# Output projection of a hybrid attention block: the second half of a row block's work comes one row block later, and the late rows' steps sit at earlier positions

## The chip, the cores and the metric

The kernel runs on one core of one Trainium2 chip, in one launch. A core has a matrix engine (TensorE, PE in the profile), three elementwise engines (VectorE is DVE, ScalarE is ACT, GpSimd is POOL) and a queue engine, SyncE (SP), which issues nearly all DMAs of this kernel. Each engine works through its own instruction list in order; semaphores tie the lists together. The metric is the device time of the whole launch in microseconds, lower is better.

## The reference

One layer of a pre-norm residual trunk over 2048 tokens of width 1024: an input projection, two groups of attention heads (four differential heads, eight stick-breaking heads), an output projection with a residual, and a SwiGLU feed-forward of width 2816 with a residual.

```python
u = rms_norm(h, norm1_w[l])
proj = jnp.einsum('bsd,de->bse', u, w_in[l])
dq, dk, dv, sq, sk, sv = jnp.split(proj, SPLIT_POINTS, axis=-1)
...
y_diff = rms_norm(y_diff, diff_out_norm_w[l]) * (1.0 - lambda_init)
...
y_sb = rms_norm(stick_breaking_attention(sq, sk, sv), sb_out_norm_w[l])
...
h = h + jnp.einsum('bse,ed->bsd', mix, w_out[l])
u2 = rms_norm(h, norm2_w[l])
gate = jnp.einsum('bsd,df->bsf', u2, w_gate[l])
up = jnp.einsum('bsd,df->bsf', u2, w_up[l])
h = h + jnp.einsum('bsf,fd->bsd', jax.nn.silu(gate) * up, w_down[l])
```

The change touches the two lines in the middle: the output projection, and the preparation of `u2` for the feed-forward.

## The kernel before

**Number form.** A float32 matrix product is computed as three float16 products: each operand is split into a high half (the rounded value) and a low half (the rest), and high·high, high·low and low·high are added up in PSUM. In the feed-forward each product of 2×2 blocks is done with seven instead of eight block products. For that the activations need seven combinations of their blocks, each one split in two halves. They are kept in DRAM (`xcd`) and loaded as seven tiles `X`, once for each half of the 2048 rows.

**Order of work.** Tokens are handled in 16 row blocks of 128. The attention is run in eight groups of heads; while the last group's attention runs, the output projection's row blocks are dealt in between (`next(op)`), each as soon as the attention of its rows is finished. After the attention come the row blocks that are left; row blocks 12 to 15 are dealt among the loads of the first feed-forward weights. Then the feed-forward runs in 22 steps, 11 groups of 256 columns (`fg`) for each half of the rows: a gate product, an up product (each a `quad` of seven block products of 12 matmuls), and after every few steps a `down` product.

The order in each engine's list is not the program's order. A scheduler simulates the engines and gives each engine, among the instructions whose inputs are ready in its simulation, the one with the highest priority; priority is the place in the program, with offsets (`PRI`; the attention's stages are moved 200 places forward, `ox` and `po` not at all). `tc.issue_after(ins)` adds an edge of order alone: the instructions made inside the block that run on the same engine as `ins` come behind it in that engine's list. Other engines are not bound by it. `note` and `pick` keep a running account of load and choose the engine of a cast or a subtraction.

**A row block of the output projection** (`out_proj`, from L816). The 2·8 halves of the mix rows are loaded (`mt`, L819) and the residual row too (`xf`, L824). Two PSUM banks `po` (a pool of two) take 48 matmuls each, in two parts of 24 (L832). After each 24, VectorE reads the part and adds it to `xf` (L835): these four instructions are the "bank reads". The row goes to DRAM (`hd`, L837).

**`post(t, xf)`** (L848), for row blocks 0 to 11. It takes two tiles of `z4` for each pair of row blocks (a ring of ZB = 9 tiles of 4 KB a partition, which the attention's stages use too, two tiles a stage). Then: norm of the row (ScalarE squares with a running sum L226, a mean L155 on VectorE, a power on POOL L156, a product on VectorE L229); eight PE transposes into two PSUM banks of the attention's tag `sc` (L665) and two ScalarE copies back (L853); and, on odd row blocks, `x_ops` for the pair: the block combinations and splits (casts L89 or L93, subtractions L98), put in `s16` tiles (a ring of three, shared with the attention's splits) and stored to `xcd` (L238), four stores a pair.

**The late rows.** Row blocks 12 to 15 do not pass through `post`. Their norm, transposes and combinations are done during the first two feed-forward steps by a generator, `build_x` (L1189), which works in 15 segments. One call of `tick` runs one segment. The first, called ahead of the steps, reads row blocks 12 and 13 back from `hd` (L1203). Then come, for the pair (12, 13): the norm, the transposes (L1213, L1214), the first put, the combinations, the second put, the third put, and the fourth put together with the read of row blocks 14 and 15; and then the same seven for the pair (14, 15). The split halves stand in a tile `b16` that belongs to the tag `act` (two tiles). The other `act` tile takes the first step's activations, and the second step's activations need the one that `b16` gives back.

`late_at` (L1256) says at which positions of the steps 0 and 1 a segment is run. Position s = 1 to 7 is behind the s-th block product of the gate, 8 to 14 behind the products of up:

```python
def row(s):
    if i < 2 and s in late_at[i]:
        tick(1)
```

In a `quad`, the read of the fourth block product (L1057, tile `c22`) must be done before the seventh, which adds to the same PSUM bank `pd`. Weights of the next step are loaded and split meanwhile (L89 to L221, L954 to L964, tiles `wg`, `wu`, `wd`, staging tile `stages`).

Of the kernel before, what the change touches and what calls it, by code (L numbers as in the profile page):

```python
# [16 lines left out]
ALU = mybir.AluOpType  # L17
# [4 lines left out]
S, D, P = 2048, 1024, 128  # L22
# [37 lines left out]
def block(tc, a, out):  # L60
    nc = tc.nc
    PE, ACT, DVE, POOL, SP = nc.tensor, nc.scalar, nc.vector, nc.gpsimd, nc.sync
    top = ExitStack()
    with top:
# [8 lines left out]
        def note(e, ns):  # L73
            load[e] += ns * KW[e]
# [25 lines left out]
        def pri(k):  # L100
            def deco(f):
                @functools.wraps(f)
                def g(*args):
                    with tc.high_priority(PRI[k]) if PRI[k] else nullcontext():
                        return f(*args)
                return g
            return deco

        def nm(s):
            uid[0] += 1  # L110
            return f"{s}{uid[0]}"
# [38 lines left out]
        def rstd(dst, ss, mul, eps):  # L150
            n = dst.shape[-1]
            if n > 1:
                ACT.activation(dst, ss, AF.Identity, bias=eps, scale=mul)
            else:
                DVE.tensor_scalar(dst, ss, mul, eps, op0=ALU.mult, op1=ALU.add)  # L155
            POOL.tensor_tensor(dst, dst, mhalf[:, :n], ALU.pow)  # L156
# [67 lines left out]
        def norm_tile(xf, xn, wgt, junk=None):  # L224
            ss = sm.tile([P, 1], F32, tag="xss", name=nm("xss"))
            ACT.activation(xn if junk is None else junk, xf, AF.Square, accum_out=ss[:])  # L226
            rs = sm.tile([P, 1], F32, tag="xrs", name=nm("xrs"))
            rstd(rs[:], ss[:], 1.0 / D, EPS)
            DVE.scalar_tensor_tensor(xn, xf, rs[:], wgt, op0=ALU.mult, op1=ALU.mult)  # L229

        def x_ops(xn, xt, half, j, bufs, engines="ADP", tte="DP"):
            def put(o, src):
                k = src.shape[1]
                x16 = bufs()
                xv = x16[:, : 1024 * k].rearrange("p (o s n) -> p o s n", o=k, s=2)
                to16(xv[:, :, 0, :], src, 512 * k, engines)
                tt(xv[:, :, 1, :], src, xv[:, :, 0, :], ALU.subtract, 512 * k, tte)
                SP.dma_start(xcd[half][o : o + k, :, j, :].rearrange("o p n -> p o n"), x16[:, : 1024 * k].rearrange("p (o n) -> p o n", o=k))  # L238

            put(0, xn[0])  # L240
            yield
            tt(xt[:, 1], xn[1][:, 1], xn[1][:, 0], ALU.subtract, 512, tte)
            tt(xn[1][:, 0], xn[1][:, 0], xn[0][:, 0], ALU.subtract, 512, tte)
            tt(xt[:, 0], xn[1][:, 1], xn[1][:, 0], ALU.subtract, 512, tte)
            tt(xn[0][:, 0], xt[:, 0], xn[0][:, 1], ALU.subtract, 512, tte)
            yield
            put(2, xn[1])
            yield
            put(4, xt)
            yield  # L250
            put(6, xn[0][:, 0:1])
# [5 lines left out]
        with ExitStack() as ph1:  # L257
# [6 lines left out]
            def z4():  # L264
                return zp.tile([P, 1028], F32, tag="z4", bufs=ZB, name=nm("z4"))
# [396 lines left out]
            def transposed(xn, o):  # L662
                tr = ps.tile([P, 512], F32, tag="sc", bufs=4, name=nm("xtr"))
                for j in range(4):
                    PE.transpose(tr[:, P * j : P * j + P], xn[:, o + P * j : o + P * j + P], id32[:])  # L665
                return tr
# [121 lines left out]
            wos, kos, mts, rp2, spare = [], [], [], [], {}  # L788
# [24 lines left out]
            w2 = bias[:].rearrange("p h n -> p (h n)")  # L813

            def out_proj():
                for t in range(NT):  # L816
                    mt = pp.tile([P, 2 * D], F16, tag="xt", bufs=3, name=nm("mt"))[:].rearrange("p (k n) -> p k n", k=KT)
                    with tc.high_priority(PRI["wm"]) if PRI["wm"] else nullcontext():
                        mts.append(SP.dma_start(mt, ms[t]))  # L819
                    if t in spare:  # L820
                        xf = spare[t].bitcast(F32)
                    else:
                        xf = pp.tile([P, 4, 4, 2, 64], F16, tag="st", name=nm("xf"))[:].rearrange("p c t s e -> p (c t s e)").bitcast(F32)
                    SP.dma_start(xf, x[t * P : (t + 1) * P, :])  # L824
                    for h in range(2):
                        po = psj.tile([P, 512], F32, tag="pj", name=nm("po"))
                        for n in range(2):
                            q = 0
                            sl = slice(256 * n, 256 * n + 256)
                            for kt in range(KT):  # L830
                                for xi, wi in ((0, 0), (0, 1), (1, 0)):
                                    PE.matmul(po[:, sl], lhsT=mt[:, kt, P * xi : P * xi + P], rhs=wos[2 * h + n][wi][:, kt, :], start=q == 0, stop=q == 23)  # L832
                                    q += 1
                            xl = xf[:, 512 * h + 256 * n : 512 * h + 256 * n + 256]
                            DVE.scalar_tensor_tensor(xl, po[:, sl], kos[2 * h + n][:], xl, op0=ALU.mult, op1=ALU.add)  # L835
                    note("D", 1400)
                    SP.dma_start(hd[t], xf)  # L837
                    if t >= 12:
                        yield
                        continue  # L840
                    post(t, xf)
                    yield

            held = []

            @pri("ox")
            def post(t, xf):
                if t % 2 == 0:  # L848
                    held[:] = [z4(), z4()]
                xn = held[t % 2]  # L850
                norm_tile(xf, xn[:, :D], w2)
                for h in range(2):
                    ACT.copy(xn[:, 512 * h : 512 * h + 512], transposed(xn, 512 * h)[:])  # L853
                note("D", 1150)
                note("A", 1000)
                if t % 2 == 1:
                    for _ in x_ops([z[:, :D].rearrange("p (d n) -> p d n", d=2) for z in held], z4()[:, :D].rearrange("p (d n) -> p d n", d=2), t // 8, t % 8 // 2, lambda: s16p.tile([P, 2048], F16, tag="s16", bufs=SB, name=nm("x16"))[:]):
                        pass

            op = out_proj()  # L860
            outs = 0
            advance(NT - LAG0)
# [11 lines left out]
        with ExitStack() as ph2:  # L874
# [378 lines left out]
            units = []  # L1253
            hs = None
            chains = {}
            late_at = ((5, 9, 10, 11, 12, 13), (1, 6, 9, 10, 11, 12, 13, 14))  # L1256
            for i, (half, fg) in enumerate(steps):
                if i == NFG:
                    load_x(1, XL)
# [83 lines left out]
```

## Time and profile before

| | us |
|---|---|
| median of 3 runs | 2685.7 (2677.81 to 2689.95) |
| the profiled execution | 2685.45 |
| its span, from the first instruction to the last | 2683.6 |
| PE busy in the span | 2498.7 (93%) |
| DVE busy | 1937.3 (72%) |
| POOL busy | 1477.3 (55%) |
| ACT busy | 1346.4 (50%) |

All times in the views are microseconds from the start of the span, single instructions' means in ns where said. A row of the timeline gives start, duration, engine, line, operation and tiles, with the idle time before it in brackets and what ended it. A row of the waits gives the engine and line that waited, what released it, the total, how often, and the longest. A row of the windows gives length, then busy time (and count) of PE, PEld, DVE, ACT and POOL, the granted PE clock, the DMA share and GB/s. Row blocks 0 to 11 lie between 1181 and 1386 us, row blocks 12 to 15 between 1386 and 1428, the first feed-forward step from 1428.4 to 1470.2, the second from there to 1518.6.

### The profile page before, as it was taken

The numbers are of one execution on the slowest core, as the hardware profiler recorded it, in microseconds if no ns is written. First come the engines' busy times: TensorE is split into PE (matmuls) and PEld (weight loads), VectorE is DVE, ScalarE is ACT, GpSimd is POOL, SyncE is SP. The second block draws the span as 40 slices with busy tenths as digits, with TensorE's granted clock in tenths as the row PEclk, the third lists the DMA queues.
The fourth block names the chain that finished last, engine by engine and source line by source line (L and its number), as shares of the span: only waits on it lengthen the run. The fifth ranks groups of instructions, "written<-read, shape, count | busy, mean of one in ns | idle before, by whom it ended". The sixth has DMA issues, their size and how long they took to land. (4 is left out here: it accounts for less than half of the span.)

```text
span 2683.6 us, 50578 instructions
## 1 busy us (share of the span) xinstructions
PE 2498.7 (93%) x19628; PEld 1503.2 (56%) x19628; DVE 1937.3 (72%) x3714; ACT 1346.4 (50%) x2487; POOL 1477.3 (55%) x1095
## 2 busy tenths in 40 slices
PE   7998989898988989889989799999999999999999
PEld 4655656577776776557775344444444444444444
DVE  6898879898989889877766968677785544444434
ACT  4665556567978878665644535344362112111121
POOL 2578667767767766546664546565654232322323
PEclk9999999999999999999999999999999999999999
DMA  7778697768999979987897565655648743635532
GB/s 230 204 163 185 140 206 169 179 147 175 198 178 179 180 158 206 212 191 216 216 280 292 205 231 197 255 222 206 243 184 337 301 174 144 235 140 185 196 111 95
DMA packets 619585, 534.41 MB, mean 199 GB/s; under 512 B 480640, under 2 KB 548224, under 8 KB 609104
## 3 DMA queue, kind: packets, MB, share of 16 engines
q1 hardware_dynamic: 617520, 529.09, 69.8%
q8 instruction: 154, 2.52, 0.4%
q0 software_dynamic: 512, 1.36, 0.2%
q14 instruction: 87, 0.71, 0.1%
q10 hardware_dynamic: 1312, 0.72, 0.1%
HBM read 261.08 MB, written 147.32 MB: 152 GB/s over the span
## 5 line engine op out<-in xcount | busy, mean ns | idle before, releaser
L98 POOL TENSOR_TENSOR s<-z,s 128x1024 f16<-128x1024 f32 (+7 forms) x288 | 471.8, 1647 | 145.0 <-ACT s L89 119.5
L507 PE MATMUL sc<-kT,qT 128*128 128x512 f16 (+3 forms) x1520 | 383.9, 355 | 53.8 <-DVE z L623 19.3
L622 DVE TENSOR_TENSOR_SCAN z<-z,sc 128x512 f32<-128x512 f32 (+3 forms) x320 | 352.9, 1112 | 61.7 <-ACT sc L620 37.3
L1138 PE MATMUL pd<-wd,act 128*128 128x512 f16 x1764 | 390.2, 379 | 0.3 <-DVE cg L1071 0.3
L326 PE MATMUL pj<-w,xt 128*128 128x384 f16 x1920 | 354.4, 333 | 14.3 <-ACT raw L375 5.8
L1030 PEld LDWEIGHTS <-wg 128*128 128x128 f16 x1848 | 182.2, 99 | 236.1 <-issue 22.9
L98 POOL TENSOR_TENSOR act<-cg,act 128x512 f16<-128x512 f32 x110 | 145.8, 1333 | 291.9 <-ACT act L1097 179.5
L518 PE MATMUL yp<-v,aT 128*128 128x64 f16 (+1 forms) x4896 | 269.7, 204 | 39.4 <-DMA aT<-s 38.4
L518 PEld LDWEIGHTS <-aT 128*128 128x128 f16 x4896 | 238.2, 99 | 117.6 <-DMA aT<-s 48.5
L1030 PEld LDWEIGHTS <-wu 128*128 128x128 f16 x1848 | 180.6, 98 | 218.4 <-DVE wu L221 3.2
L1138 PEld LDWEIGHTS <-act 128*128 128x128 f16 x1764 | 172.5, 98 | 207.9 <-issue 0.6
L326 PEld LDWEIGHTS <-xt 128*128 128x128 f16 x1920 | 188.2, 100 | 144.5 <-issue 23.4
L89 ACT CAST s<-z 128x128 f16<-128x128 f32 (+7 forms) x215 | 173.1, 809 | 137.5 <-DMA aT<-s 43.3
L98 POOL TENSOR_TENSOR hs<-hs,cu 128x512 f32<-128x512 f32 x99 | 132.0, 1340 | 171.4 <-DVE hs L1144 70.3
L619 ACT ACTIVATE z<-sc,c 128x512 f32<-128x512 f32 (+3 forms) x320 | 210.7, 663 | 28.7 <-PE sc L507 14.4
L1097 ACT CAST act<-cg 128x512 f16<-128x512 f32 x126 | 77.1, 617 | 242.0 <-DVE cg L1103 193.5
L507 PEld LDWEIGHTS <-qT 128*128 128x128 f16 x1520 | 128.7, 99 | 122.5 <-DVE z L623 22.8
L832 PE MATMUL po<-wo,mt 128*128 128x256 f16 x1536 | 181.0, 277 | 14.1 <-DVE xf L835 8.4
L342 PE MATMUL pj<-xt,w 128*128 128x128 f16 x2304 | 177.5, 222 | 6.7 <-DVE v L364 5.7
L1030 PE MATMUL pm<-X,wu 128*128 128x512 f16 x792 | 180.1, 379 | 2.2 <-DVE wu L221 2.2
L1030 PE MATMUL pm<-X,wg 128*128 128x512 f16 x792 | 178.9, 379 | 0.0
L1144 DVE SCALAR_TENSOR_TENSOR hs<-pd,c,hs 128x512 f32<-128x512 f32 x136 | 98.8, 747 | 110.1 <-PE pd L1138 81.8
(267 smaller groups left out, 4739.5 us busy)
## 6 DMA issues: line engine op xcount, KB each, us to landing
xt<-xs SPq DMA_DIRECT2D x112, 512.0 KB, 4.4
hs<-hd SPq DMA_DIRECT2D x68, 512.0 KB, 4.5
hd<-hs SPq DMA_DIRECT2D x56, 512.0 KB, 4.8
split<-wg SPq DMA_DIRECT2D x11, 1792.0 KB, 7.1
split<-wu SPq DMA_DIRECT2D x11, 1792.0 KB, 7.4
split<-wd SPq DMA_DIRECT2D x11, 1792.0 KB, 6.9
wg<-split SPq DMA_DIRECT2D x11, 1792.0 KB, 7.6
wd<-split SPq DMA_DIRECT2D x11, 1792.0 KB, 10.3
```

The source lines that it names most:

```text
L89: ACT.copy(dst, src)
L98: (DVE if e == "D" else POOL).tensor_tensor(dst, a_, b_, op)
L326: PE.matmul(pj[:, :384], lhsT=xv[:, xi, kt, :], rhs=G["w"][:, wi, kt, :], start=n == 0, stop=n == 23)
L342: PE.matmul(o, lhsT=x_ if c == 2 else w_, rhs=w_ if c == 2 else x_, start=n == 0, stop=n == 23)
L507: last = PE.matmul(sc[:, : 128 * w].rearrange("p (t n) -> p t n", n=P), lhsT=G["q"][i // 4][:, a_, i % 4, :], rhs=G["k"][q][:, b_, 0:w, :] ...
L518: PE.matmul(yp[:, y0 : y0 + wd], lhsT=aT[:, a_, :], rhs=v[:, v_ : v_ + wd], start=start and j == 0 and q == 0, stop=stop and j == nb - 1 a ...
L619: ACT.activation(om[:, lo:hi], sc[:, :w], AF.Sigmoid, scale=G["nkz"][:])
L622: DVE.tensor_tensor_scan(ov, ov, sc[:, :w], om[:, hi : hi + 1], op0=ALU.mult, op1=ALU.bypass)
L832: PE.matmul(po[:, sl], lhsT=mt[:, kt, P * xi : P * xi + P], rhs=wos[2 * h + n][wi][:, kt, :], start=q == 0, stop=q == 23)
L1030: front[0] = PE.matmul(ps_[:].rearrange("p (t n) -> p t n", n=P), lhsT=wv[:, wo, wi, 128 * kt : 128 * kt + 128], rhs=X[xo][:, :, xi, kt, : ...
L1138: front[0] = PE.matmul(po[:], lhsT=act[:, ao, xi, 128 * j : 128 * j + 128], rhs=W["d"][:, wo, wi, :], start=start and u == 0 and q == 0, s ...
L1144: DVE.scalar_tensor_tensor(dst, po[:], kd[:], src, op0=ALU.mult, op1=ALU.add)
```

## The change

`post` keeps the norm. The transposes, the copies back and, on odd row blocks, the combinations and splits move into a new function, `post_late`. Row block t, once its own bank reads are traced, runs `post_late(t - 1)` and then `post(t)`; the VectorE instructions of `post_late` are tied behind row block t's last bank read (`seen`). Row block 11 runs its own `post_late` at once behind its `post`. Row blocks 12 to 15 still have neither.

`late_at` puts eleven of the fourteen segments into step 0 (six before) and three into step 1 (eight before), the last at position 4 of step 1 (14 before).

```diff
-                            DVE.scalar_tensor_tensor(xl, po[:, sl], kos[2 * h + n][:], xl, op0=ALU.mult, op1=ALU.add)
+                            seen = DVE.scalar_tensor_tensor(xl, po[:, sl], kos[2 * h + n][:], xl, op0=ALU.mult, op1=ALU.add)
                     note("D", 1400)
                     SP.dma_start(hd[t], xf)
-                    if t >= 12:
-                        yield
-                        continue
-                    post(t, xf)
+                    if 0 < t < 12:
+                        with tc.issue_after(seen.ins):
+                            post_late(t - 1)
+                    if t < 12:
+                        post(t, xf)
+                    if t == 11:
+                        post_late(t)
                     yield
...
             def post(t, xf):
                 if t % 2 == 0:
                     held[:] = [z4(), z4()]
+                norm_tile(xf, held[t % 2][:, :D], w2)
+
+            @pri("ox")
+            def post_late(t):
                 xn = held[t % 2]
-                norm_tile(xf, xn[:, :D], w2)
                 for h in range(2):
                     ACT.copy(xn[:, 512 * h : 512 * h + 512], transposed(xn, 512 * h)[:])
...
-            late_at = ((5, 9, 10, 11, 12, 13), (1, 6, 9, 10, 11, 12, 13, 14))
+            late_at = ((1, 3, 4, 5, 6, 7, 8, 10, 12, 13, 14), (1, 2, 4))
```

## The prediction, on record before the changed kernel was run

> **What bounds the kernel now.** I read the page first, then the busy time by stage, then PE's waits in the stages that the change touches, then the timeline around the longest of them.
>
> ```profile
> span 2683.6 us, 50578 instructions
> PE 2498.7 (93%) x19628; PEld 1503.2 (56%) x19628; DVE 1937.3 (72%) x3714; ACT 1346.4 (50%) x2487; POOL 1477.3 (55%) x1095
> ```
>
> ```profile
> 1181.00:1386.00 205.00, 190.66 (x2031) 160.83 (x2030) 151.07 (x235) 120.50 (x204) 129.63 (x86) 0.97 0.81 211
> 1386.00:1428.20 42.20, 36.73 (x332) 32.16 (x330) 24.71 (x42) 13.28 (x13) 22.97 (x16) 1.00 1.03 400
> 1428.20:1548.50 120.30, 103.20 (x490) 49.09 (x489) 98.61 (x134) 65.87 (x84) 63.72 (x43) 0.94 0.60 216
> ```
>
> PE bounds the kernel, so the change can win only what PE idles, and what it runs slowed, where the change acts. The three stages are row blocks 0 to 11, row blocks 12 to 15, and the feed-forward from its first gate to the end of its third. PE idles 205 − 190.7 = 14.3 us in the first and 17.1 us in the third, where its clock is also lowest (0.94). Its waits there:
>
> ```profile
> PE po L832 <- DVE xf L835: 8.4, 6, 3.7
> PE sc L507 <- ACT z L853: 1.0, 3, 0.5
> ```
>
> ```profile
> PE pd L1030 <- DVE cg L1057: 12.0, 2, 6.2
> PE fsc L963 <- ACT sq L954: 2.7, 1, 2.7
> PE pd L1030 <- DVE cu L1057: 1.4, 1, 1.4
> ```
>
> The first fence is row blocks 0 to 11, the second the feed-forward's start. In both, VectorE is late in freeing a PSUM bank. It is busy 151.1 of 205 us and 98.6 of 120.3 us, so the question is mostly what stands ahead of a bank read in its list.
>
> **The row blocks: what is moved.** These instructions come one row block later:
>
> ```profile
> L665 PE MATMUL xtr<-id,z 128*128 128x128 f32 x96 | 14.2, 274 | 1.4 <-DVE z L229 1.4
> ```
>
> ```profile
> L853 ACT COPY z<-xtr x24: 578/586/626, 1220.6 to 1385.6; 128x512 f32<-128x512 f32 x24
> L238 SPq DMA_DIRECT2D xcd<-x x24: 319/371/1507, 1234.6 to 1399.5; - x24
> L1225 SPq DMA_DIRECT2D X<-xcd x14: 319/382/963, 1382.9 to 2064.1; - x14
> ```
>
> 96 transposes (14.2 us of PE), 24 copies, the casts and subtractions of six pairs, and 24 stores in SP's list. Nothing is removed: all of it stays work and counts as nothing in the sum. What can change is what waits. `issue_after` adds no instruction.
>
> ```profile
> 1266.12 2.29 DVE L98 TENSOR_TENSOR z<-z,z 128x512 f32<-128x512 f32 x1
> 1331.10 1.20 DVE L98 TENSOR_TENSOR x<-z,x 128x1024 f16<-128x1024 f32 x1
> ```
>
> ```profile
> 1234.75 9.12 PE L832 MATMUL po<-wo,mt 128*128 128x256 f16 x82
> 1268.86 10.25 PE L832 MATMUL po<-wo,mt 128*128 128x256 f16 x66 [3.73 <-DVE xf L835]
> 1334.51 2.78 PE L832 MATMUL po<-wo,mt 128*128 128x256 f16 x24 [1.21 <-DVE xf L835]
> ```
>
> A combination of the pair before (2.29 us) ran straight ahead of the bank read for which PE waited 3.73 us. After that wait 66 matmuls took 10.25 us; at 9.12/82 = 0.111 us each they take 7.3, so the slowed clock cost another 2.9. A split (1.20 us) runs ahead of the wait of 1.21. Behind the last bank read such work does no harm: both banks are then just freed, and PE has up to 48 matmuls for one bank, 48 × 0.111 = 5.3 us, before it misses the next. The transposes' wait for the norm (1.4) goes, since the norm is then a row block old. The score matmuls' wait for the copies (1.0) should go too, since the copies need not wait for a norm either. That is at most 3.73 + 2.9 + 1.2 + 1.4 + 1.0 = 10.2 us. The other bank-read waits (8.4 − 4.9 = 3.5 us) have attention's instructions, a norm, or a late load ahead of them, and the norm stays where it was. I take three quarters of 10.2, **7.5 us**, because a list made anew will have new collisions; bounds 13.7 (10.2 and the 3.5) and a loss, priced as the slow rival below.
>
> The Trainium skill (TensorE: Matmul & The Clock Gate, Part 1) says that an idle window of about 3.4 us halves PE's clock until a busy window of that length has passed. By it a long stall costs an estimated 1.7 us on top of itself, where the row gives 2.9; with 1.7 the row blocks' maximum would be 9.0.
>
> Row block 11's two halves now stand close to row block 10's: two more copies (0.59 us each) come ahead of the last pair's work. They lie beside the matmuls of row blocks 12 to 15 (36.7 of 42.2 us PE). I count nothing; without that cover it is 1.2 us. A cast for which `pick` now takes another engine is also off PE's path; the rows above bound the difference by about one subtraction, 1.2 us either way. The stores pass row loads in SP's list, 0.37 us each; a load held up behind one costs that much, and the `X` tiles that need them are first loaded at 1382.9.
>
> **The late rows: what goes.** The last store out of `b16` gives back the tile that step 1's activations need.
>
> ```profile
> 1521.03 0.43 SPq L238 DMA_DIRECT2D xcd<-b  x1
> 1528.07 1.66 ACT L1097 CAST act<-cg 128x512 f16<-128x512 f32 x3 [4.06 <-DMA xcd<-b]
> 1536.18 3.42 DVE L98 TENSOR_TENSOR act<-cg,act 128x512 f16<-128x512 f32 x2
> ```
>
> ```profile
> 1526.15 2.75 PE L1030 MATMUL pa<-X,wg 128*128 128x512 f16 x12
> 1531.59 1.03 PE L963 MATMUL fsc<-sq,ones 128*128 128x256 bf16 x8 [2.68 <-ACT sq L954]
> 1544.04 4.63 PE L1030 MATMUL pd<-X,wg 128*128 128x512 f16 x12 [6.24 <-DVE cg L1057]
> ```
>
> ScalarE stands 4.06 us for that store. Behind it in its list stand the squares of the next weight, for which PE waits 2.68 us; behind the casts stand VectorE's subtractions, and these come ahead of the bank read for which PE waits 6.24 us. After that the matmuls are slowed, 4.63 − 2.75 = 1.9 us. Together 10.8 us. With the last segment at position 4 of step 1 instead of 14, some ten products of 2.6 us earlier, the tile is back before the activations ask for it. I take all **10.8**; the lower bound is nothing, if VectorE's queue and not the tile sets that stall.
>
> **What the late rows cost.** They come into a stretch in which VectorE is already late.
>
> ```profile
> 1485.69 2.04 DVE L229 SCALAR_TENSOR_TENSOR bx<-bx,xrs,bx 128x1024 f32<-128x1024 f32 x1
> 1487.66 3.48 DVE L221 SCALAR_TENSOR_TENSOR wu<-stages,c,wu 128x1024 f16<-128x1024 f32 x2
> 1491.72 0.68 DVE L1057 TENSOR_TENSOR cg<-pd,cg 128x512 f32<-128x512 f32 x1
> ...
> 1506.77 0.68 DVE L98 TENSOR_TENSOR bx<-bx 128x512 f32<-128x512 f32 x1
> 1507.55 2.43 DVE L98 TENSOR_TENSOR bx<-bx,bx 128x512 f32<-128x512 f32 x1
> 1511.38 1.74 DVE L98 TENSOR_TENSOR bx<-bx,bx 128x512 f32<-128x512 f32 x1
> 1515.57 2.29 DVE L98 TENSOR_TENSOR b<-bx,b 128x1024 f16<-128x1024 f32 x1
> ```
>
> ```profile
> 1492.45 4.82 PE L1030 MATMUL pd<-X,wg 128*128 128x512 f16 x12 [5.73 <-DVE cg L1057]
> ```
>
> In step 1's gate PE waits 5.73 us for a read that stands behind a norm and a weight split. The norm leaves that place, but the second pair's combinations, 0.68 + 2.43 + 1.74 + 2.29 = 7.1 us, move from behind this wait to before it. Bounds: +7.1, if all of it lands ahead of the read; −2.0, if only the norm's going is felt. I take half of 7.1, **3.6 us of loss**, because part of it fills gaps that VectorE has in step 0.
>
> How early can they start?
>
> ```profile
> 1437.41 2.58 SPq L1203 DMA_DIRECT2D bx<-hd  x2
> 1471.25 0.41 SPq L1203 DMA_DIRECT2D bx<-hd  x1
> ```
>
> ```profile
> 1447.89 1.06 ACT L226 ACTIVATE bx<-bx 128x1024 f32<-128x1024 f32 x1 [3.05 <-DMA bx<-hd]
> ```
>
> The first pair's rows land at 1447.9, when gate 0 (seven products of some 2.6 us from 1428.4) is over, so positions 1, 3 and 4 of step 0 can bring nothing forward before that; ScalarE already stands 3.05 us for them. Gain and loss begin with the pair's combinations and with the second read (1471.25), which I expect some 5 us earlier. Should the scheduler put the squares further ahead, the gate's ScalarE work stands behind the same landing; PE's next bank is freed by VectorE, so I count nothing, and 3.05 more if that cover is gone. The four stores and two reads of the second pair pass weight loads in SP's list at about 0.4 us each, with the DMA share at 0.60: nothing.
>
> The Trainium skill (SBUF — State Buffer, "SBUF: two separate sides") says that VectorE with two SBUF inputs and GpSimd lock each other out of a shared port for a whole instruction. The same 128x512 subtraction takes 0.68 and 2.43 us in the rows above. By that rule it matters what POOL runs beside the moved work: if all four ran at 0.68 to 1.2 the loss above would be an estimated 2 us less, if each met a POOL instruction it would be as counted.
>
> **The sum.** 7.5 + 10.8 − 3.6 = 14.7 us. The profiled execution took 2685.45, almost the runs' median of 2685.7, so the forecast is 2685.45 − 14.7 = **2671 us**. Its own range, with the row blocks at 4 to 10.2 and the late rows at 3.7 to 10.8, is 2664.5 to 2677.8.
>
> **The rivals.**
> *All of it* (chance 0.16): both stretches lose nearly all idle time: 13.7 from the row blocks, 10.8 from the later stall, and 5.73 + 2.1 (4.82 − 2.75) from the earlier one: 32.3 us, 2653; about 2660 when a quarter stays. For it: VectorE is not full in either stretch (74% and 82%). Against: at 82% it has little room for order to help.
>
> *It does not do what it says* (0.20): the scheduler places by readiness, the transposes were already behind the norm, and the tile is given back early but VectorE's backlog only changes its place. Then the row blocks give half (4), the late rows 4.06 − 7.1 = −3: 2684.
>
> *Slower, by tiles* (0.25): a pair now keeps its two `z4` tiles until a row block later, so that while a pair is combined five of nine are held (two old, one scratch, two new) instead of three, and attention has four, two stages, instead of six, three stages.
>
> ```profile
> L610 DVE COPY z<-z x14: 136/144/146, 1187.9 to 1352.2; 128x1 f32<-128x1 f32 x14
> L608 DVE MEMSET z<- x13: 59/59/59, 1182.8 to 1335.0; 128x1 f32 x13
> ```
>
> 27 stages start between 1182.8 and 1352.2, one per 6.5 us. If each of the four pairs combined in that time costs attention one stage, that is 26 us; half covered by PE's row matmuls, 13. The row blocks then gain nothing, the late rows keep 7.2: 2691 to 2704, likeliest 2700 since the row blocks still to come need the attention's rows. It decides once score matmuls wait longer for PE than the 5.3 us that a bank covers. For it: the ring is shared. Against: no row of before shows a wait for a `z4` tile, and the new pair's norm can wait a row block.
>
> **How the numbers follow.** Forecast 0.39, all 0.16, nothing 0.20, slower 0.25. A measurement of this kernel tells 0.5% from no change: 2672.3 and 2699.1. Faster: 0.16 + 0.25 of the forecast's 0.39 = 0.41. Slower: 0.21 of the 0.25. Same: 0.38. The range, 2653 to 2702, reaches from the full gain to the middle of the slow rival and leaves out some 0.15.
>
> **What would show it.** In the changed profile: PE's wait for L835 in the row blocks at 5 us or less, with no L98 straight ahead of a bank read; transposes with no wait for L229; the last `xcd<-b` issued before 1510, no wait of ScalarE for it, and the wait of 6.24 gone; the wait of step 1's gate up by about 3.6. Wrong would be: PE waiting for scores or for `aT` by 10 us or more in the row blocks (the tiles), or a wait at L1057 that grows by over 7.

## The result, and the profile after

| | median (us) | range of the runs | runs |
|---|---|---|---|
| before | 2682.27 | 2677.81 to 2689.95 | 5 |
| changed | 2697.81 | 2691.70 to 2700.85 | 5 |

The ratio, taken over the single runs and not from the two medians, is 1.0048, with a 95% interval of 1.0032 to 1.0063: slower by 12.9 us (8.6 to 16.9). The medians lie 15.5 us apart. The forecast was 2671, so the sign is wrong. The time stands inside the range, near its slow end.

The profiled execution of the changed kernel took 2691.70 us, the lowest of its five; that of before took 2685.45, above its median. The two traces therefore show 6.3 us of the difference. Most of what is missing lies ahead of the change: the first matmul of row block 0 (L832) starts at 1176.7 us in the changed kernel's trace and at 1181.3 in before's, though nothing ahead of it was changed. Over the fourteen traces of this document it starts between 1174.0 and 1185.5. Counted from that matmul to the end, the pair shows 10.9 us. From L853 on the changed kernel's lines are 6 higher: L1057 is now L1063, L1213 is L1219, L954 is L960.

The page of the changed kernel first, then its busy time by stage (row blocks 0 to 11; the feed-forward's start), then before's row for the same stretch of the feed-forward:

```profile
span 2689.9 us, 50570 instructions
PE 2492.7 (93%) x19628; PEld 1498.9 (56%) x19628; DVE 1927.6 (72%) x3709; ACT 1348.9 (50%) x2489; POOL 1479.3 (55%) x1098
```

```profile
1181.00:1386.00 205.00, 187.07 (x2010) 157.77 (x2009) 142.22 (x221) 116.11 (x195) 129.32 (x87) 0.98 0.77 208
1430.00:1550.00 120.00, 99.94 (x486) 49.77 (x485) 81.41 (x118) 59.83 (x77) 59.32 (x40) 0.93 0.58 212
```

```profile
1430.00:1550.00 120.00, 102.90 (x487) 48.81 (x486) 97.84 (x128) 67.37 (x84) 63.72 (x43) 0.94 0.60 216
```

In the feed-forward's start VectorE has become much less busy (81.4 of 120 us against 97.8), and still PE idles 20.1 us there, where it idled 17.1. That points away from a VectorE that has too much to do. PE's waits from 1432 to 1560 say what the new idle time is:

```profile
PE xtr L1219 <- DVE bx L229: 11.4, 1, 11.4
PE pd L1036 <- DVE cg L1063: 7.9, 2, 4.1
...
```

One wait of 11.4 us is new: the transposes of row blocks 12 and 13 wait for the norm. PE's timeline around it, and the other engines' at the same time:

```profile
1437.06 2.75 PE L1036 MATMUL pa<-X,wg 128*128 128x512 f16 x12 [0.67 <-ACT cg L1049]
1451.22 3.74 PE L1219 MATMUL xtr<-id,bx 128*128 128x128 f32 x16 [11.41 <-DVE bx L229]
1454.80 2.75 PE L1036 MATMUL pd<-X,wg 128*128 128x512 f16 x12
...
1476.39 1.91 PE L1219 MATMUL xtr<-id,bx 128*128 128x128 f32 x16
...
1504.02 5.28 PE L1036 MATMUL pd<-X,wg 128*128 128x512 f16 x12 [4.12 <-DVE cg L1063]
...
1548.75 2.75 PE L1036 MATMUL pd<-X,wg 128*128 128x512 f16 x12 [3.81 <-DVE cg L1063]
1551.92 1.46 PE L1144 MATMUL pd<-wd,act 128*128 128x512 f16 x6 [0.42 <-ACT cg L1089]
```

```profile
1440.43 0.86 SPq L1209 DMA_DIRECT2D bx<-hd  x2
1447.88 1.06 ACT L226 ACTIVATE bx<-bx 128x1024 f32<-128x1024 f32 x1 [10.87 <-DMA bx<-hd]
1449.88 1.28 DVE L229 SCALAR_TENSOR_TENSOR bx<-bx,xrs,bx 128x1024 f32<-128x1024 f32 x1 [0.66 <-POOL xrs L156]
```

An engine's timeline is its list, since it issues in that order. PE finishes a product at 1437.06 + 2.75 = 1439.81 and has the sixteen transposes next. The rows are asked for at 1440.43 and have landed by 1447.88, as in before's trace; ScalarE's squares and VectorE's product follow, and PE goes on at 1451.22. The fourth product of the gate (`pd` at 1454.80) stands behind the transposes. It needs neither the rows nor the norm: right behind the transposes it runs with no wait. The stall costs another 3.74 − 1.91 = 1.8 us by the slowed clock, against the second pair's same sixteen. Together 13.2 us.

What the positions give back is in the same rows: the two waits for the fourth product's read are 7.9 us instead of 12.0, the wait of 2.68 for the squares is gone, and the 4.63 us product is back at 2.75. So the first `down` product, at 1548.50 before, begins 3.4 us later and not 13. (The 4.6 us by which this trace's row blocks began earlier had been used up by their end.) The other 2.9 of the traces' 6.3 us come behind it, mostly in one more wait for a fourth product's read after 1560, first the changed kernel, then before:

```profile
PE pd L1036 <- DVE cg L1063: 4.9, 1, 4.9
```

```profile
PE pd L1030 <- DVE cg L1057: 2.7, 1, 2.7
```

PE's waits in the row blocks, 1180 to 1390, of the changed kernel; behind it two rows of the same view of before, that the prediction did not show:

```profile
PE po L832 <- DVE xf L835: 5.3, 6, 1.2
PE sc L507 <- DVE z L623: 4.0, 5, 1.5
PE xtr L665 <- DVE z L608: 2.4, 1, 2.4
PE yp L518 <- DMA aT<-s: 2.3, 2, 1.3
PE xtr L665 <- DVE z L229: 1.9, 2, 1.2
```

```profile
PE sc L507 <- DVE z L623: 1.7, 2, 1.5
...
PE yp L518 <- DMA aT<-s: 0.9, 1, 0.9
```

The bank reads' wait went from 8.4 to 5.3 and the longest from 3.7 to 1.2, as the change is built to do. But the score matmuls now wait 4.0 us for the attention's VectorE work (1.7 before), the transposes 2.4 for an attention instruction (none before), `aT` comes 2.3 us late (0.9). The 3.1 us that the output projection won stand against 2.3 + 2.4 + 1.4 = 6.1 us that the work beside it lost.

### The profile page after: what moved, and what is told of

The parts are those of the page before. It is cut to its first block, busy times and chain, and to the rows that moved or that the text cites. A ratio compares the mean times of both kernels' runs of the same rounds, so it can differ in the third digit from the quotient of the medians.

```text
span 2689.9 us, 50570 instructions
## 1 busy us (share of the span) xinstructions
PE 2492.7 (93%) x19628; PEld 1498.9 (56%) x19628; DVE 1927.6 (72%) x3709; ACT 1348.9 (50%) x2489; POOL 1479.3 (55%) x1098
## 5 line engine op out<-in xcount | busy, mean ns | idle before, releaser
L98 POOL TENSOR_TENSOR s<-z,s 128x1024 f16<-128x1024 f32 (+7 forms) x288 | 469.7, 1640 | 153.5 <-ACT s L89 121.6
L98 POOL TENSOR_TENSOR act<-cg,act 128x512 f16<-128x512 f32 x112 | 147.4, 1325 | 293.9 <-ACT act L1103 181.7
L98 POOL TENSOR_TENSOR hs<-hs,cu 128x512 f32<-128x512 f32 x99 | 132.0, 1340 | 171.4 <-DVE hs L1150 69.7
L832 PE MATMUL po<-wo,mt 128*128 128x256 f16 x1536 | 184.4, 279 | 8.8 <-DVE xf L835 5.3
## 6 DMA issues: line engine op xcount, KB each, us to landing
wd<-split SPq DMA_DIRECT2D x11, 1792.0 KB, 10.8
```

Of the source, the lines that this page charges most:

```text
L98: (DVE if e == "D" else POOL).tensor_tensor(dst, a_, b_, op)
```

## The experiments

The theory after the two traces: the row blocks bring nothing either way, and the loss is PE standing at the first pair's transposes, because positions 1 and 3 put them ahead of a product that could run. The rivals: the row blocks lose it through the `z4` tiles, or the whole crowd of late steps loses it through VectorE. Every ratio is against runs of before that were taken along with it on the same chip. The medians of before in these four sets of runs were 2684.2, 2681.5, 2684.5 and 2679.7, so ratios count, not times.

### Each half alone

e1: the changed row blocks with the old positions.

```diff
-            late_at = ((1, 3, 4, 5, 6, 7, 8, 10, 12, 13, 14), (1, 2, 4))
+            late_at = ((5, 9, 10, 11, 12, 13), (1, 6, 9, 10, 11, 12, 13, 14))
```

> The row blocks' half of the change alone, with the positions of the late rows as before. Theory (the loss comes from the positions: the first pair's transposes stand in PE's list ahead of gate 0's fourth product and wait for the rows' return): PE never waits 11 us for L229, time 2676 to 2684, that is -6 to +2 us against before. Rival (the loss comes from the row blocks, by tiles held longer or by row block 15's end coming 6 us later): +8 to +15 us.

Measured: 2685.19 (12 runs), ratio 1.0001 [0.9988, 1.0014]. PE's waits in the row blocks, 1181 to 1390:

```profile
PE po L832 <- DVE xf L835: 5.3, 6, 1.2
PE yp L518 <- DMA aT<-s: 3.4, 3, 2.0
PE sc L507 <- DVE z L623: 3.0, 6, 0.9
...
```

By these runs the row blocks' half is neutral: a gain above 0.12% (3.2 us) and a loss above 0.14% (3.8 us) are both outside the interval. The shorter bank reads are there, and so are the waits that eat them. The traces lean to a small loss. From the first to the last matmul of the output projection (L832) the eight traces with the old row blocks take 246.4 to 249.0 us and the six with the changed ones 257.9 to 260.7. In these six, 30 matmuls of the first gate (6.5 us) run inside that stretch; what is left is some 5 us more on average. Part of it comes back later: from that first matmul to the end of the kernel, the four pairs of traces that differ in the row blocks alone show 0.4 to 5.3 us. The `z4` rival falls: nothing here is near its 13 us.

e2: the old row blocks with the new positions, the same edit the other way round.

> The positions of the late rows alone, row blocks as before. Theory: PE waits some 11 us for L229 in gate 0, and the time is 10 to 18 us above before. Rival (row blocks): within 4 us of before.

Measured: 2695.60 (5 runs), ratio 1.0042 [1.0027, 1.0058], which is the changed kernel within the intervals. PE's waits in the feed-forward's start:

```profile
PE xtr L1213 <- DVE xrs L155: 11.1, 1, 11.1
PE pd L1030 <- DVE cg L1057: 8.0, 2, 4.2
```

The loss is in the positions. (The releaser is named L155 here and L229 there: the transposes wait for VectorE's part of the norm, in which both stand.)

### Which positions

What a position does to PE's list stands in the code. The late transposes are made inside `with behind():`, and `behind()` is `tc.issue_after(front[0])`, where `front[0]` is the last matmul of the product traced just before. So position s ties the transposes behind the s-th product, and behind nothing later. In before (position 9) the first pair's follow the ninth product directly, at 1453.73.

e3: only the first pair's norm and transposes are moved, from positions 5 and 9 to 1 and 3.

```diff
-            late_at = ((5, 9, 10, 11, 12, 13), (1, 6, 9, 10, 11, 12, 13, 14))
+            late_at = ((1, 3, 10, 11, 12, 13), (1, 6, 9, 10, 11, 12, 13, 14))
```

> Before, with only the first two segments (the first pair's norm and transposes) moved from positions 5 and 9 to 1 and 3. Theory (it is these two alone): PE waits some 11 us for L229, +8 to +15 us. Rival (VectorE is crowded by the second pair's segments): within 4 us of before, no long wait for L229.

Measured: 2691.63 (12 runs), ratio 1.0029 [1.0018, 1.0040]. PE's timeline:

```profile
1452.58 3.99 PE L1213 MATMUL xtr<-id,bx 128*128 128x128 f32 x16 [11.11 <-DVE xrs L155]
```

Two numbers of fourteen bring the whole wait, and 0.29 of the 0.42%. The remaining 0.13% would be the other steps', but the intervals of e2 and e3 overlap, so that is not shown. No run moves the first pair's norm alone; the second pair's stands at position 1 in e9 and e11 below, and they lose nothing.

e4: the complement; the first pair stays behind the gate, the second pair goes to positions 1 to 7 of step 1.

```diff
+            late_at = ((5, 9, 10, 11, 12, 13, 14), (1, 2, 3, 4, 5, 6, 7))
```

> Before, with the first two segments at 5 and 9 as they were and all later ones pulled forward (step 0: 5, 9 to 14; step 1: 1 to 7). Theory, with the prediction's term for the tile given back early: no ScalarE wait for the last xcd store, the 6.2 us wait at the bank read of step 2's gate gone, -4 to -10 us. Rival (VectorE's backlog sets that wait and only moves): -2 to +6 us.

Measured: 2683.15 (12 runs), ratio 1.0005 [0.9992, 1.0017]. PE's timeline:

```profile
1494.04 1.94 PE L1213 MATMUL xtr<-id,bx 128*128 128x128 f32 x8 [7.92 <-DVE bx L229]
1499.22 1.97 PE L1213 MATMUL xtr<-id,bx 128*128 128x128 f32 x8 [3.24 <-DVE bx L229]
...
1551.86 4.44 PE L1030 MATMUL pd<-X,wg 128*128 128x512 f16 x12 [3.11 <-DVE cg L1057]
```

The mechanism returns one step later: position 2 of step 1's gate puts the second pair's transposes ahead of products, and PE stands 11.2 us for their norm. This time the ratio shows no loss, and not the gain of 4 us or more that was expected either: the waits of 5.73 and 2.68 us are gone and the 6.24 is down to 3.11. VectorE had PE's 11.2 us of standing to catch up in, so this trace can't say whether the tile or the pause took them away.

### Why the fourth product stands behind the transposes

In the changed kernel's timeline above, the program's fifth product (the second `pa`, at 1437.06) runs ahead of the transposes and its fourth (`pd`) behind them. The fifth adds to a PSUM bank that is already held. The fourth needs a new one, and so do the transposes: one each for the four halves of a pair's two rows, from the same pools (`pst`). `behind()` allows position 3's transposes ahead of the fourth product; what puts them there is the scheduler. The theory was that it gives out banks in the program's order.

e5: the changed kernel with one bank for a pair's four halves, used one after another.

```diff
+                    tr = pst("xtr")
                     for z in (xa, xb):
                         for h in range(2):
-                            tr = pst("xtr")
```

> The changed kernel, with the four late transposed halves of a pair passing through one PSUM bank in turn instead of taking four. Theory (the four tiles are placed ahead of gate 0's fourth product and take its bank, so that PE must do the transposes first): in PE's list the fourth product comes ahead of the transposes, PE's wait of 11.4 us for L229 shrinks to under 4, and the time is 8 to 14 us below the changed kernel, 2682 to 2690. Rival (the scheduler simply takes the rows to be back by then): the transposes stay ahead, the wait stays at 10 to 12, the time at 2692 to 2700.

Measured: 2697.82 (5 runs), ratio 1.0061 [1.0047, 1.0074]. PE's timeline:

```profile
1441.98 2.75 PE L1036 MATMUL pd<-X,wg 128*128 128x512 f16 x12
...
1448.72 2.76 PE L1036 MATMUL pd<-X,wg 128*128 128x512 f16 x12 [1.39 <-DMA X<-xcd]
...
1458.16 0.60 PE L1219 MATMUL xtr<-id,bx 128*128 128x128 f32 x4
...
1497.16 1.08 PE L1219 MATMUL xtr<-id,bx 128*128 128x128 f32 x4 [18.08 <-DVE xrs L155]
```

With three banks fewer, six of the gate's seven products run ahead of the first pair's transposes, both on `pd` among them, and the wait is gone. That bears out the banks for this place. The time missed its expectation, because the second pair's first four transposes now stand ahead of six of the seven products of step 1's gate, and PE waits 18.1 us for their norm. The trace shows why that norm is so late. One bank lets only four transposes pass at a time, so the first pair's last four end at 1473.9 instead of 1455.0; the second pair's rows, which are read into the first pair's tiles, come later with them:

```profile
1493.73 1.06 ACT L226 ACTIVATE bx<-bx 128x1024 f32<-128x1024 f32 x1 [2.04 <-DMA bx<-hd]
```

In the changed kernel these squares start at 1471.63, 22 us earlier, while the transposes that need them stand only three products (7.8 us) further back in PE's list.

e6: two banks, one for each row block (`tr = pst("xtr")` one line lower).

> The changed kernel, with two PSUM banks for a pair's four late transposed halves, one for each row block. Theory (banks): the first row block's four transposes still stand ahead of the fourth product; they need the first row block's norm alone, so PE waits 8 to 11 us, and the time lies 0 to 4 us below the changed kernel. Rival (the scheduler's idea of the rows' return): as with four banks, 10 to 12 us.

Measured: 2711.37 (4 runs), ratio 1.0106 [1.0092, 1.0120]. PE's timeline:

```profile
1455.70 1.11 PE L1219 MATMUL xtr<-id,bx 128*128 128x128 f32 x4 [11.66 <-DVE xrs L155]
...
1498.67 1.09 PE L1219 MATMUL xtr<-id,bx 128*128 128x128 f32 x4 [8.65 <-DVE xrs L155]
```

Both pairs now stall, 20.3 us in all, and the time is far above the expectation. With two, the first four transposes still stand ahead of the fourth product in the first gate, and the second gate stalls as with one: the second pair's squares start at 1495.24.

e7: four banks, before's code, the first pair's transposes at position 4, that is behind the fourth product.

```diff
+            late_at = ((1, 4, 10, 11, 12, 13), (1, 6, 9, 10, 11, 12, 13, 14))
```

> The kernel before, with the first pair's norm at position 1 and its transposes at position 4 (run three had them at 1 and 3), all else as before. The fourth product is now traced ahead of the transposes and has its bank. Theory: six of gate 0's seven products run ahead, PE comes to the transposes some 5 us later than with position 3, waits 5 to 8 us for L229 instead of 11, and the time is 2 to 7 us above before. Rival (moving them at all crowds VectorE): the same time as with position 3, +8 us.

Measured: 2688.15 (7 runs), ratio 1.0023 [1.0012, 1.0034]. PE's timeline:

```profile
1443.33 4.45 PE L1030 MATMUL pd<-X,wg 128*128 128x512 f16 x12 [3.54 <-DMA X<-xcd]
1449.76 1.25 PE L1213 MATMUL xtr<-id,bx 128*128 128x128 f32 x8 [1.98 <-DVE xrs L155]
```

One position later both products on `pd` run first, and the wait falls from 11.1 to 2.0 us. A loss of 0.23% (6.2 us) is left, and its interval overlaps e3's. In the trace the sixth product still stands behind the first eight transposes. So PE comes to the seventh one product earlier and waits 3.54 us for its `X` tile (0.96 before), then 1.98 for the norm, and two products run slowed (4.45, and 4.32 at 1450.81, instead of 2.75). Together that is 2.6 + 2.0 + 3.3 = 7.9 us, enough for the loss.

e8: e4 with one bank as in e5.

> The kernel before with the later segments pulled forward as in run four (5, 9 to 14; 1 to 7), and one PSUM bank for a pair's transposed halves. Run four lost the tile's gain again to 11.2 us of waiting for L229 at the second pair. Theory: that wait falls under 4 us, the tile's gain stays, 5 to 10 us faster than before. Rival (VectorE's backlog): the wait turns up at bank reads (L1057) instead, -2 to +4 us.

Measured: 2691.07 (5 runs), ratio 1.0041 [1.0028, 1.0054]. PE's timeline:

```profile
1480.89 1.03 PE L1030 MATMUL pa<-X,wu 128*128 128x512 f16 x2 [5.64 <-ACT wu L216]
1495.91 1.11 PE L1213 MATMUL xtr<-id,bx 128*128 128x128 f32 x4 [5.88 <-DVE xrs L155]
```

Fewer banks make e4 worse. The second pair's wait is 5.9 instead of 11.2 us, but an up product now comes so early that its weights are not split yet (5.64). Banks decide the order in the first gate. For the second pair fewer of them also make its rows late: counted from row block 0's first matmul, its squares start at 318.3 us here and at 300.9 in e4. Why the scheduler does not place its transposes later then stays open.

### Every transpose behind its gate

If the clash is the cause, positions behind a gate should lose nothing, and show what giving the tile back early is worth. e9 moves the second pair's transposes to position 7 of step 1, e11 to position 8; e10 and e12 are the same two with the changed row blocks.

```diff
+            late_at = ((5, 9, 10, 11, 12, 13, 14), (1, 7, 8, 9, 10, 11, 12))
+            late_at = ((5, 9, 10, 11, 12, 13, 14), (1, 8, 9, 10, 11, 12, 13))
```

> The kernel before with the later segments pulled forward, but each pair's transposes left where its rows are back: first pair 5 and 9 as before, second pair's norm at position 1 of step 1 and its transposes at 7, the last segment at 12 (14 before, 4 in the changed kernel). Theory (the tile's gain is real, and was lost to transposes standing ahead of their rows): PE's wait for L229 under 4 us in all, no ScalarE wait for the last xcd store, the wait of 6.2 us in step 2's gate halved or gone, -3 to -9 us. Rival (VectorE's backlog): -2 to +4 us, the wait turning up at another bank read.

Measured: 2687.08 (12 runs), ratio 1.0004 [0.9990, 1.0017]. PE's waits, 1432 to 1560:

```profile
PE pd L1030 <- DVE cg L1057: 5.5, 1, 5.5
PE pd L1138 <- DVE cg L1071: 3.8, 1, 3.8
PE pd L1138 <- ACT cg L1083: 3.2, 1, 3.2
...
```

No wait for a norm is left. The later wait at L1057 is gone, and 7.0 us of waits of the `down` product stand in its place, as the rival said: the wait turns up elsewhere.

> The changed kernel's row blocks with the positions of run nine. Theory (row blocks neutral): within 3 us of run nine. Rival (the row blocks' new order makes the start of the feed-forward later): 4 to 8 us above run nine.

Measured: 2685.31 (12 runs), ratio 1.0005 [0.9995, 1.0016]: the row blocks add nothing here either.

> As run nine with the second pair's segments one product later (transposes at 8, the last at 13). Theory: -2 to -8 us, within 3 us of run nine, wait for L229 smaller than in run nine. Rival: as before, within 2 us.

Measured: 2680.35 (12 runs), ratio 0.9982 [0.9970, 0.9995]. PE's waits, then rows of the timeline: SP's last stores out of `b16`, VectorE ahead of the later wait's end, and the product behind it:

```profile
PE pd L1030 <- DVE cg L1057: 12.3, 2, 6.9
...
```

```profile
1517.41 0.88 SPq L238 DMA_DIRECT2D xcd<-b  x2
...
1534.99 1.45 DVE L98 TENSOR_TENSOR act<-cg,act 128x512 f16<-128x512 f32 x2
...
1538.93 1.29 DVE L221 SCALAR_TENSOR_TENSOR wu<-stages,c,wu 128x1024 f16<-128x1024 f32 x1 [0.62 <-ACT wu L216]
1540.13 0.69 DVE L1057 TENSOR_TENSOR cg<-pd,cg 128x512 f32<-128x512 f32 x1
1540.87 4.10 PE L1030 MATMUL pd<-X,wg 128*128 128x512 f16 x12 [6.87 <-DVE cg L1057]
```

The last store is out some 3 us before the 1521.03 of before, ScalarE's activations no longer wait for it, and the squares' wait of 2.68 is gone. The wait at L1057 stays, 6.87 instead of 6.24: ahead of the read stand the activations' subtractions and a weight split. It is VectorE's backlog, not the tile. Before's own trace held the sign of it, in VectorE's row behind the casts that waited 4.06 us for the store:

```profile
1528.72 1.29 DVE L98 TENSOR_TENSOR act<-cg,act 128x512 f16<-128x512 f32 x2 [1.35 <-ACT act L1097]
```

VectorE stood only 1.35 us for them; the rest of the time it had other work. e11 met its expected gain, but not the expectation that it lies within 3 us of e9.

> The changed row blocks, with the positions of e11 (first pair from position 5 of step 0, second pair's transposes behind position 8 of step 1) in place of the change's. If the whole loss of the change is in its positions and the row blocks are neutral whatever follows them, this is e11 again: 2679 to 2683 on a before of 2684.5, ratio 0.998, no wait for L229 or L155 in the feed-forward's first two steps, the wait at L1063 near 12. If the two halves of the change are not independent (row blocks that end later push the late rows' reads), the time is above 2686.

Measured: 2680.83 (11 runs), ratio 1.0003 [0.9993, 1.0013]; PE's waits in the feed-forward's start:

```profile
PE pd L1036 <- DVE cg L1063: 12.5, 2, 6.8
```

The waits are e11's and the time is e11's, but before was 4.7 us faster in this set of runs, and the ratio missed its expectation. So e11's 0.18% is the only result below before whose interval excludes 1, and the run most like it doesn't repeat it. No version here is shown to be better than before.

## Why the prediction was wrong

**The step that failed** is the sentence on the late rows' start: "positions 1, 3 and 4 of step 0 can bring nothing forward before that … Gain and loss begin with the pair's combinations". The landing was right (1447.88), and that moving the norm forward doesn't bring the rows earlier. Wrong was what followed: that a step which can't begin earlier is harmless earlier. Its instructions are in the lists from its position on. I asked that of ScalarE's squares ("3.05 more") and did not ask it of the sixteen transposes, which I priced nowhere in the late rows. PE had three of gate 0's products still to run, and stood 11.4 us ahead of them. With the slowed transposes that is 13.2 us, where the prediction has nothing. e3 shows the wait from those two positions alone; e7 shows it shrink with a position further back. e9 and e11 show a second pair without it.

**Row blocks, −7.5: measured about 0** (e1: a gain of 3.2 at most, a loss of 3.8 at most). The mechanism was right: 8.4 to 5.3, the 3.7 us wait gone. The size failed: the term counted the "new collisions" as a quarter of its gain, where they were all of it. Three of its parts did not come either: transposes still wait 1.9 us for L229 (1.4 before), the score matmuls 1.4 for the copies (1.0 before), and splits (L98) still stand straight ahead of bank reads, for one of which PE waits 0.6 us.

**The tile, −10.8: mis-sized.** The waits of 4.06 and 2.68 went, as traced. The 6.24 and its slowed product, 8.1 us of the term, did not go for that reason: in e11, where no cast waits for the store, they are 6.87 and 4.10 − 2.75 = 1.4. The lower bound that the prediction named, "if VectorE's queue and not the tile sets that stall", is what the run showed. In the changed kernel this wait is 3.81, with PE 13 us held back earlier.

**Crowding, +3.6: not where it was put.** Step 1's gate wait fell from 5.73 to 4.12 and was 5.47 in e11. Waits came in other places: 4.9 instead of 2.7 us after 1560 (4.9 in e2 too, 2.7 in e3 and e4), and the `down` product's waits in e9; that these are its price is not shown. The term was also read a little high: of its four rows the last, 2.29 us, is a split and no combination.

**The rivals.** "Slower, by tiles" gave 2691 to 2704, which holds the time, but e1 leaves no room for its 13 us. That the range holds the measured time is luck: its slow end was there for the tiles. "Does not do what it says" was partly right on the tile. "All of it" was far off. None of them was an in-order engine held by work that is early in its list.

**The signs.** Right: the last `xcd<-b` at 1495.66 (before 1510), ScalarE's wait for it gone. Nearly: L835 at 5.3, asked 5. Wrong: no L98 straight ahead of a bank read (three are left, at 1274.57, 1346.25 and 1349.08), transposes without a wait for L229, the wait of 6.24 gone (3.81 is left), the gate wait up by 3.6. The prediction's own signs of failure, 10 us more at scores and `aT` or 7 at L1057, did not come: what failed had no sign set for it.

**Open.** Counted from row block 0's first matmul, the traces and the ratios agree to within some 5 us: 10.9 and 12.9 for the pair, 6.2 and 7.8 for e3, 10.5 and 11.3 for e2; the widest gap is e1's, 5.3 and 0.3. Whether the changed row blocks cost a few us or none lies inside that gap. Open too is why the scheduler put transposes where their rows could not be back: the list shows where it put them, not what it took the landing to be.

## What to carry to other kernels

Moving a step forward in a program whose engines issue in order moves every instruction of it, on every engine. Before counting a step as "can't start earlier, so no harm", find what stands behind its first instruction on each engine, the bottleneck engine first, and price that work waiting for the step's slowest input. And a wait that is taken away on one of two interleaved streams is only a gain once the other stream's waits have been seen not to grow.

## What the runs showed of the hardware

What a stall costs PE behind it does not go by the stall's length alone. One row of e3's timeline:

```profile
1539.14 1.87 PE L963 MATMUL fsc<-sq,ones 128*128 128x256 bf16 x8 [3.06 <-ACT sq L954]
```

After 3.06 us these eight matmuls took 1.87 us instead of 1.03, and after 3.11 us (e4, 1551.86) a product took 4.44 instead of 2.75. After 3.81 us (the changed kernel, 1548.75) a product ran at its 2.75. The cost does not grow with the stall: 1.8 us in the row behind 11.41 and 2.5 in the one behind 4.12 (both in the changed kernel), 1.7 behind e4's 3.11. The Trainium skill (TensorE: Matmul & The Clock Gate, Part 1) lets PE fall to half its clock after an idle window of about 3.4 us that runs freely, not from the stall's begin. The cost that doesn't grow agrees with it; the slowed rows below 3.4 us don't, and there the measurement decides.
